# RWKV heads of a hybrid trunk: one standing PSUM tile for two banks, and output products in one queue behind the state update

## The chip, the cores and the metric

The kernel runs on one core of one Trainium2 chip. The metric is the device time of one execution in microseconds. The program uses TensorE (PE in the profile, its weight loads PEld), VectorE (DVE), ScalarE (ACT), GpSimd (POOL) and the DMA queues issued by SyncE (SP).

## The reference

One layer of a hybrid trunk over 4096 tokens of width 1024: h = RMSNorm(x), one projection of h whose columns feed three head groups, the group outputs concatenated, one output projection, RMSNorm, residual add.

- Mamba-2 group: 8 heads of 64, causal convolution, chunked scan, gated norm.
- RWKV-7 group: 4 heads of 64. Per head and token `S = S * w + (S a) b^T + v k^T` and `y = S r`, then a GroupNorm over the 64 channels of a head, a bonus and a SiLU gate.
- Memory attention group: 4 heads of 64 over 256 memory tokens.

```python
def step(S, inp):
    r_t, w_t, k_t, v_t, a_t, b_t = inp
    sa = jnp.einsum('bhij,bhj->bhi', S, a_t)
    S = S * w_t[:, :, None, :] + sa[..., None] * b_t[:, :, None, :] + v_t[..., None] * k_t[:, :, None, :]
    return S, jnp.einsum('bhij,bhj->bhi', S, r_t)
```

The change touches the RWKV group and the PSUM banks that the other two groups share with it.

## The kernel before

The tokens go in 16 stages of 256 (`NS = 16`, `NT = 256`). Three phases follow one another and overlap a little at their borders: phase A does the norm, the Mamba projections and the Mamba scan, phase B the RWKV projections and recurrence, phase C the attention, the output projection and the residual. Projections are split into a high and a low part in a reduced-precision fp32 format (three products for one, in `proj_cm`, L137, and `proj_tm`, L147); all else is plain fp32, and each plain fp32 product leaves two MATMUL records in the trace.

The RWKV recurrence is computed in chunks of 64 tokens, four per stage (`NC_`). Four heads lie as two pairs `p_`; the two heads `h` of a pair are the two halves of the 128 partitions. Per stage:

- `gram2` (L722) multiplies the stacked vectors of each chunk with each other, per head over that head's 64 rows (L730), into two PSUM banks, one for each head of the pair, and VectorE masks each bank into `AT` (L733). This is done for one pair, then for the other.
- `solve2` (L741) inverts small triangular blocks with many 32x32 products (L785, L793, L805, L815) into `TT`.
- `tokmaj` (L825) copies v, r and the scaled vectors into token-major tiles: `UV`, `rr` (L840) and `BKt` (L848).
- `stage3` (L861) is the recurrence: per chunk three groups of four products one after the other, L878, L885 and L895, with copies on ScalarE and VectorE in between (L871, L881, L890), and the state update `ST` on VectorE (L898). After every second chunk (a half stage) it emits 16 output products: step 0 multiplies the state with `rr` per head over 64 rows (L912), step 1 adds the product inside the chunk (L915).
- `stage4` (L922) is the GroupNorm: per head bank a mean (L927) and a subtraction (L931) out of PSUM.

There are eight PSUM banks: two for transposes (`tr`), two for projections (`pj`), one each for `g`, `yo`, `yd` and `st`. `yd` and `st` are the two head banks of `gram2` and of the output products. Phase A uses the same two for its scan (L425 and L417), phase C for the output projection (L1165).

`weave` (L95) runs generators in turns, by the numbers given with them, and so sets the order in which instructions are traced. A list scheduler of the language then sets the order on each engine from that order, the dependencies and its own timing model. An instruction without a dependency on its neighbour can therefore land anywhere between others. PE, DVE and ACT then run their own lists in that order. A PE product is described below by its shape, rows*columns of the array that it uses, as the profile prints it: 128*128 for projections, 128*64 for L878, L895 and L915, 64*64 for L885 and L912, 64*128 for L730 and 32*32 for the solve.

Of the kernel before, what the change touches and what calls it, by code (L numbers as in the profile page):

```python
# [7 lines left out]
F32 = mybir.dt.float32  # L8
# [6 lines left out]
P = 128  # L15
# [12 lines left out]
def tile_hymba_trunk(  # L28
# [17 lines left out]

    def psum(tag, bufs):
        return ps.tile([P, 512], F32, name="ps_" + tag, tag=tag, bufs=bufs)
# [444 lines left out]
    def phase_b(a_tail, a_l):  # L493
# [216 lines left out]
        nct = bi.tile([P, 16, 2 * NPC], F32, name="nct")  # L710
# [8 lines left out]
        rr = bw.tile([P, 2, NC_, C], F32, name="rr")  # L719
        el = bw.tile([P, 2, NC_], F32, name="el")  # L720

        def gram2(i, r):  # L722
            AR, BK, ec = r["AR"], r["BK"], r["ec"]
            AT = bi.tile([P, NPC, 2, P], F32, name="AT", tag="AT", bufs=2)
            for p_ in range(2):
                pas = (psum("g", 1), ps_tr()) if i == NS - 1 else (psum("yd", 1), psum("st", 1))
                for c_ in range(NC_):
                    for h, pa in enumerate(pas):
                        hs = slice(h * 64, h * 64 + 64)
                        te.matmul(pa[:, c_ * P:(c_ + 1) * P], lhsT=BK[hs, p_, c_].rearrange("p a t -> p (a t)"),  # L730
                                  rhs=AR[hs, p_, c_].rearrange("p a t -> p (a t)"), start=True, stop=True)
                for h, pa in enumerate(pas):
                    v.tensor_tensor(out=AT[:, p_ * NC_:(p_ + 1) * NC_, h, :], in0=pa.rearrange("p (x t) -> p x t", t=P),  # L733
                                    in1=amask.unsqueeze(1).broadcast_to([P, NC_, P]), op=ALU.mult)
                    yield

                g.tensor_tensor(out=BK[:, p_].rearrange("p c a t -> p c (a t)"), in0=BK[:, p_].rearrange("p c a t -> p c (a t)"),
                                in1=ec[:, p_].unsqueeze(2).broadcast_to([P, NC_, 2 * C]), op=ALU.mult)
            r.update(scaled=True, AT=AT)

        def solve2(i, r):  # L741
            AT = r["AT"]
            for q in range(4):
# [33 lines left out]
            Dt = bi.tile([P, NPC, 32], F32, name="Dt", tag="Dt")  # L777
# [47 lines left out]
        def tokmaj(r, c2):  # L825
# [14 lines left out]
            s.copy(out=rr[:, :, cs, :], in_=AR[:, :, cs, 1, :])  # L840
# [20 lines left out]
        def stage3(i, r, nxt=None):  # L861
# [3 lines left out]
            for c_ in range(NC_):  # L865
# [26 lines left out]
                for p_, pc in enumerate(pcs):  # L892
                    for h in range(2):
                        hs = slice(h * 64, h * 64 + 64)
                        te.matmul(pch[hs, 256 + p_ * C:256 + p_ * C + C], lhsT=BKt[:, pc, hs], rhs=UV[:, pc, h, :],  # L895
# [5 lines left out]
                if c_ % 2 == 1:  # L901
                    for step in range(2):
                        for p_ in range(2):
                            for h in range(2):
                                hs = slice(h * 64, h * 64 + 64)
                                for par in range(2):
# [4 lines left out]
                                    if step == 0:  # L911
                                        te.matmul(yo, lhsT=rr[hs, p_, cq, :], rhs=sts[cq][hs, p_, :], start=(p_ == 0), stop=False,  # L912
                                                  skip_group_check=True)
                                    else:
                                        te.matmul(yo, lhsT=AT[:, pc, h, C:2 * C], rhs=UV[:, pc, h, :], start=False, stop=True,  # L915
                                                  skip_group_check=True)
# [5 lines left out]
        def stage4(i, r):  # L922

            pys = r["py"]
            mean = bw.tile([P, 2, 4], F32, name="mean", tag="mean")
            for h in range(2):
                v.tensor_reduce(out=mean[:, h, :], in_=pys[h][:, 0:256].rearrange("p (c t) -> p c t", t=C), axis=AX.X, op=ALU.add)  # L927
            g.tensor_scalar(out=mean, in0=mean, scalar1=1.0 / C, scalar2=None, op0=ALU.mult)
            yc = bw.tile([P, NPC, C], F32, name="yc", tag="yc")
            for h in range(2):  # L930
                v.tensor_tensor(out=yc[:, h::2, :], in0=pys[h][:, 0:256].rearrange("p (c t) -> p c t", t=C),  # L931
                                in1=mean[:, h, :].unsqueeze(2).broadcast_to([P, 4, C]), op=ALU.subtract)
# [354 lines left out]
```

## Time and profile before

| what | us |
|---|---|
| median of 3 runs | 2287.77 (2286.9 to 2288.61) |
| the profiled execution | 2286.42 |
| its span | 2284.7 |
| PE busy | 2211.9 (97%) |
| DVE busy | 1444.0 (63%) |
| ACT busy | 1153.6 (50%) |
| first gram product (L730) | at 821.7 |
| last transposition of the RWKV output (L946) | at 1620.2 |

Busy shares come from the records of each engine. Records of PE overlap: a product is recorded until its results are out, while the next one has started. So the time that a product takes from the others is read from start to start and not from its duration. Idle time of an engine stands with what released it.

### The profile page before, as it was taken

The numbers are of one execution on the slowest core, as the hardware profiler recorded it, in microseconds if no ns is written. First come the engines' busy times: TensorE is split into PE (matmuls) and PEld (weight loads), VectorE is DVE, ScalarE is ACT, GpSimd is POOL, SyncE is SP. The second block draws the span as 40 slices with busy tenths as digits, with TensorE's granted clock in tenths as the row PEclk, the third lists the DMA queues.
The fourth block names the chain that finished last, engine by engine and source line by source line (L and its number), as shares of the span: only waits on it lengthen the run. The fifth ranks groups of instructions, "written<-read, shape, count | busy, mean of one in ns | idle before, by whom it ended". The sixth has DMA issues, their size and how long they took to land.

```text
span 2284.7 us, 54434 instructions
## 1 busy us (share of the span) xinstructions
PE 2211.9 (97%) x22497; PEld 2091.5 (92%) x22497; DVE 1444.0 (63%) x3298; ACT 1153.6 (50%) x2803; POOL 721.0 (32%) x1047
## 2 busy tenths in 40 slices
PE   4999999999999889999999999999999999999997
PEld 4999999999999889899898899988899999999997
DVE  5788888888888986677677777776533333323322
ACT  6555555545554655666666666676423323323322
POOL 1343444343433342333433343333121212211212
PEclk8999999999999999999999999999999999999999
DMA  6232223222332422111111111234524324324311
GB/s 199 84 137 96 93 94 136 97 93 94 128 105 103 128 69 75 48 43 43 43 67 56 48 43 43 73 110 144 185 94 147 116 89 148 116 89 147 117 47 56
DMA packets 83766, 219.60 MB, mean 96 GB/s; under 512 B 9207, under 2 KB 45502, under 8 KB 71230
## 3 DMA queue, kind: packets, MB, share of 16 engines
q1 hardware_dynamic: 82334, 215.59, 27.4%
q8 instruction: 177, 2.90, 0.5%
q10 hardware_dynamic: 1184, 0.53, 0.1%
q14 instruction: 71, 0.58, 0.1%
HBM read 152.52 MB, written 63.57 MB: 95 GB/s over the span
## 4 chain that ended last, share of the span: by engine, by line
PE 85%; DVE 5%; DMA 4%; ACT 2%; issue 1%; POOL 1%; SPq 0%; POOLq 0%; DVEq 0%; ACTq 0%
PE ps_pj L137 39%; PE ps_pj L147 8%; PE ps_st L147 8%; PE ps_yd L147 8%; PE ps_pj L1140 3%; DMA w_st<-in_w_in_dram 1%; PE ps_yd L425 1%; DVE cc L296 1%; PE ps_yo L878 1%; PE ps_tr L1128 1%; PE ps_yd L730 1%; PE ps_tr L126 1%; PE ps_st L417 1%; PE ps_yo L404 1%; PE ps_st L730 1%
## 5 line engine op out<-in xcount | busy, mean ns | idle before, releaser
L137 PE MATMUL ps_pj<-hh,w_hi 128*128 128x256 f32 x2704 | 789.2, 292 | 5.7 <-ACT w_hi L78 4.0
L137 PE MATMUL ps_pj<-hh,w_lo 128*128 128x256 f32 x2704 | 778.7, 288 | 2.0 <-DVE w_lo L79 1.9
L137 PE MATMUL ps_pj<-hl,w_hi 128*128 128x256 f32 x2704 | 778.0, 288 | 0.0
L137 PEld LDWEIGHTS ps_pj<-hh,w_hi 128*128 128x128 f32 x2704 | 519.4, 192 | 15.1 <-ACT w_hi L78 4.8
L137 PEld LDWEIGHTS ps_pj<-hh,w_lo 128*128 128x128 f32 x2704 | 519.1, 192 | 8.6 <-DVE w_lo L79 3.3
L137 PEld LDWEIGHTS ps_pj<-hl,w_hi 128*128 128x128 f32 x2704 | 519.4, 192 | 7.9 <-issue 2.2
L296 DVE SCALAR_TENSOR_TENSOR cc<-ux,cwh,cc 128x256 f32<-128x256 f32 x384 | 220.1, 616 | 15.2 <-ACT cc L293 11.3
L147 PE MATMUL ps_pj<-w_hi,hh 128*128 128x260 f32 (+1 forms) x528 | 155.4, 295 | 21.5 <-DVE dtr L270 17.2
L1174 POOL TENSOR_TENSOR sq<-sq 128x1 f32<-128x1 f32 x32 | 6.2, 194 | 496.5 <-ACT ot L1172 496.5
L147 PE MATMUL ps_pj<-w_hi,hl 128*128 128x260 f32 (+1 forms) x528 | 152.3, 289 | 0.0
L147 PE MATMUL ps_pj<-w_lo,hh 128*128 128x260 f32 (+1 forms) x528 | 151.3, 287 | 0.0
L147 PEld LDWEIGHTS ps_pj<-w_hi,hh 128*128 128x128 f32 x528 | 101.7, 193 | 24.0 <-issue 17.3
L147 PEld LDWEIGHTS ps_pj<-w_lo,hh 128*128 128x128 f32 x528 | 101.5, 192 | 0.2
L147 PEld LDWEIGHTS ps_pj<-w_hi,hl 128*128 128x128 f32 x528 | 101.4, 192 | 0.0
L1180 POOL TENSOR_TENSOR xr<-ot,xr 128x512 f32<-128x512 f32 x64 | 88.0, 1398 | 26.3 <-DVE ot L1179 26.3
L299 ACT ACTIVATE th<-cc 128x512 f32<-128x512 f32 x64 | 40.4, 632 | 104.1 <-DVE cc L296 101.9
L1179 DVE SCALAR_TENSOR_TENSOR ot<-ps_yd,sq,pnw 128x512 f32<-128x512 f32 x32 | 24.0, 751 | 104.9 <-POOL sq L1176 104.9
L1093 DVE TENSOR_TENSOR ylo<-yl,yh 128x512 fp32r<-128x512 f32 x48 | 35.5, 741 | 84.4 <-ACT yh L1092 84.1
L567 ACT ACTIVATE tt<-ps_pj,omu 128x256 f32<-128x256 f32 x144 | 68.1, 473 | 38.0 <-PE ps_pj L137 25.3
L385 POOL TENSOR_TENSOR xde<-xdt,de 128x512 f32<-128x512 f32 x32 | 46.7, 1459 | 123.3 <-DVE xdt L383 119.1
L147 PE MATMUL ps_yd<-wo0h,yh 128*128 128x256 f32 x256 | 75.8, 296 | 4.2 <-DVE ot L1179 2.8
L1144 DVE TENSOR_TENSOR sg<-ps_pj,sg 128x256 f32<-128x256 f32 x32 | 13.6, 424 | 104.0 <-PE ps_pj L1140 104.0
(453 smaller groups left out, 5891.4 us busy)
## 6 DMA issues: line engine op xcount, KB each, us to landing
hl<-hTd SPq DMA_DIRECT2D x32, 1024.0 KB
hh<-hTd SPq DMA_DIRECT2D x32, 1024.0 KB
xt<-in_x_dram SPq DMA_DIRECT2D x32, 512.0 KB
hTd<-hh SPq DMA_DIRECT2D x16, 1024.0 KB
hTd<-hl SPq DMA_DIRECT2D x16, 1024.0 KB
R<-rowd SPq DMA_DIRECT2D x32, 512.0 KB
xr<-in_x_dram SPq DMA_DIRECT2D x32, 512.0 KB
out_dram<-xr SPq DMA_DIRECT2D x32, 512.0 KB
```

Source lines behind the costliest of these rows:

```text
L126: te.transpose(pt[:, q * P:(q + 1) * P], src[:, k * P:(k + 1) * P], ident)
L137: te.matmul(outp, lhsT=a[:, k, :], rhs=b[:, k, :], start=(n == 0), stop=(n == 3 * KB - 1))
L147: te.matmul(outp, lhsT=a[:, k, tsl], rhs=b[:, k, 0:ncol], start=(n == 0), stop=(n == 3 * KB - 1))
L296: v.scalar_tensor_tensor(out=cc[:, b_, :], in0=ux[:, b_, j:j + NT], scalar=wj(j), in1=cc[:, b_, :], op0=ALU.mult, op1=ALU.add)
L299: s.activation(out=th, in_=cc, func=AF.Tanh)
L385: g.tensor_tensor(out=h3(xde), in0=h3(xdt), in1=b3(q[c]["de"]), op=ALU.mult)
L567: s.activation(out=tt[:, b_, :], in_=pv[:, b_, :], func=AF.Copy, scale=omu[:, m0 + b_:m0 + b_ + 1])
L730: te.matmul(pa[:, c_ * P:(c_ + 1) * P], lhsT=BK[hs, p_, c_].rearrange("p a t -> p (a t)"), rhs=AR[hs, p_, c_].rearrange("p a t -> p (a t)" ...
L1093: v.tensor_tensor(out=YL[:, bs, :], in0=yl, in1=YH[:, bs, :].bitcast(F32), op=ALU.subtract)
L1140: te.matmul(po[g_ * 64:g_ * 64 + 64, p_ * P:(p_ + 1) * P], lhsT=vm[:, m_, n_ * 64:n_ * 64 + 64], rhs=pT[:, p_, m_, :], start=(m_ == 0), st ...
L1179: v.scalar_tensor_tensor(out=ots[n_], in0=pos[n_], scalar=sq[:, 0:1], in1=pnw[:, cs], op0=ALU.mult, op1=ALU.mult)
L1180: g.tensor_tensor(out=xr[:, cs], in0=ots[n_], in1=xr[:, cs], op=ALU.add)
```

## The change

The two tags `yd` and `st` no longer come from the rotating pool. One tile `big` of two banks is allocated once, and `psum("yd", ...)` and `psum("st", ...)` return its two halves, in all three phases. With it:

- `gram2` masks both banks with one VectorE instruction over 1024 elements per partition, except in the last stage, which uses other banks.
- `stage4` takes the means with one reduction and subtracts with one instruction.
- `rr` is twice as large and cleared once; each head's r is copied into its own half of the partitions and its own slot, so that the other half of the rows is zero. The state product then contracts over all 128 rows.
- State product and output product of one destination follow each other, and all 16 of a half stage are traced inside `tc.issue_after(upd.ins)`: they stand behind the last product of the state update (L895 before, L908 now) on PE's list.
- `nct` and `Dt` take the buffers of `N` and `T`, which makes room.

```diff
+    big = ps.tile([P, 2, 512], F32, name="ps_big")
     def psum(tag, bufs):
+        if tag in ("yd", "st"):
+            return big[:, ("yd", "st").index(tag), :]
         return ps.tile([P, 512], F32, name="ps_" + tag, tag=tag, bufs=bufs)
...
-        nct = bi.tile([P, 16, 2 * NPC], F32, name="nct")
...
-        rr = bw.tile([P, 2, NC_, C], F32, name="rr")
+        rr = bw.tile([P, 2, 2, NC_, C], F32, name="rr")
+        v.memset(rr, 0.0)
...
-                for h, pa in enumerate(pas):
-                    v.tensor_tensor(out=AT[:, p_ * NC_:(p_ + 1) * NC_, h, :], in0=pa.rearrange("p (x t) -> p x t", t=P),
-                                    in1=amask.unsqueeze(1).broadcast_to([P, NC_, P]), op=ALU.mult)
-                    yield
+                if i == NS - 1:
...
+                else:
+                    v.tensor_tensor(out=AT[:, p_ * NC_:(p_ + 1) * NC_].rearrange("p x h t -> p h x t"),
+                                    in0=big.rearrange("p h (x t) -> p h x t", t=P),
+                                    in1=amask.unsqueeze(1).unsqueeze(1).broadcast_to([P, 2, NC_, P]), op=ALU.mult)
+                yield
+                yield
...
+            nct = bi.tile([P, 16, 2 * NPC], F32, name="nct", tag="N")
...
-            Dt = bi.tile([P, NPC, 32], F32, name="Dt", tag="Dt")
+            Dt = bi.tile([P, NPC, 32], F32, name="Dt", tag="T")
...
-            s.copy(out=rr[:, :, cs, :], in_=AR[:, :, cs, 1, :])
+            for h in range(2):
+                hs = slice(h * 64, h * 64 + 64)
+                s.copy(out=rr[hs, h, :, cs, :], in_=AR[hs, :, cs, 1, :])
...
-                        te.matmul(pch[hs, 256 + p_ * C:256 + p_ * C + C], lhsT=BKt[:, pc, hs], rhs=UV[:, pc, h, :],
+                        upd = te.matmul(pch[hs, 256 + p_ * C:256 + p_ * C + C], lhsT=BKt[:, pc, hs], rhs=UV[:, pc, h, :],
                                   start=True, stop=True)
...
-                    for step in range(2):
+                    with tc.issue_after(upd.ins):
                         for p_ in range(2):
                             for h in range(2):
-                                hs = slice(h * 64, h * 64 + 64)
                                 for par in range(2):
...
-                                    if step == 0:
-                                        te.matmul(yo, lhsT=rr[hs, p_, cq, :], rhs=sts[cq][hs, p_, :], start=(p_ == 0), stop=False,
-                                                  skip_group_check=True)
-                                    else:
-                                        te.matmul(yo, lhsT=AT[:, pc, h, C:2 * C], rhs=UV[:, pc, h, :], start=False, stop=True,
-                                                  skip_group_check=True)
+                                    te.matmul(yo, lhsT=rr[:, h, p_, cq, :], rhs=sts[cq][:, p_, :], start=True, stop=False)
+                                    te.matmul(yo, lhsT=AT[:, pc, h, C:2 * C], rhs=UV[:, pc, h, :], start=False, stop=True)
...
-            for h in range(2):
-                v.tensor_reduce(out=mean[:, h, :], in_=pys[h][:, 0:256].rearrange("p (c t) -> p c t", t=C), axis=AX.X, op=ALU.add)
+            pyv = big[:, :, 0:256].rearrange("p h (c t) -> p h c t", t=C)
+            v.tensor_reduce(out=mean, in_=pyv, axis=AX.X, op=ALU.add)
...
-            for h in range(2):
-                v.tensor_tensor(out=yc[:, h::2, :], in0=pys[h][:, 0:256].rearrange("p (c t) -> p c t", t=C),
-                                in1=mean[:, h, :].unsqueeze(2).broadcast_to([P, 4, C]), op=ALU.subtract)
+            v.tensor_tensor(out=yc.rearrange("p (c h) t -> p h c t", h=2), in0=pyv,
+                            in1=mean.unsqueeze(3).broadcast_to([P, 2, 4, C]), op=ALU.subtract)
```

How the order on PE moves: this is PE's list before at the end of the second chunk pair of a stage in the middle of phase B (`ps_yd` and `ps_st` are the two head banks, `ps_yo` the chunk's bank, `ps_pj` a projection's; the last numbers are partitions x elements of the result).

```order
L137 MATMUL ps_pj<-hl,w_hi 128x256
L912 MATMUL ps_yd<-ST,rr 64x64
L137 MATMUL ps_pj<-hh,w_lo 128x256
L912 MATMUL ps_st<-ST,rr 64x64
L912 MATMUL ps_yd<-ST,rr 64x64
L912 MATMUL ps_st<-ST,rr 64x64
L912 MATMUL ps_yd<-ST,rr 64x64 x2
L912 MATMUL ps_st<-ST,rr 64x64
L878 MATMUL ps_yo<-UV,AT 64x64 x4
L912 MATMUL ps_st<-ST,rr 64x64
L915 MATMUL ps_yd<-UV,AT 64x64
L915 MATMUL ps_st<-UV,AT 64x64
```

The eight state products stand in three pieces with a projection product and a chunk group in between, and two of the eight output products behind them; the other six follow in two pieces further on. Now the list of the change at the same place of a stage (its lines are 4 higher in the projections, 13 higher at the state update, and L923 and L924 stand for L912 and L915):

```order
L141 MATMUL ps_pj<-hl,w_hi 128x256
L141 MATMUL ps_pj<-hh,w_lo 128x256
L908 MATMUL ps_yo<-UV,BKt 64x64 x4
L923 MATMUL ps_big<-ST,rr 64x64
L924 MATMUL ps_big<-UV,AT 64x64
```

The last two rows repeat until each stands eight times, and then projection products follow. No other product stands between the state update and the last of the sixteen.

On DVE, before, around the masking of the gram products of a stage:

```order
L733 TENSOR_TENSOR AT<-ps_yd,amask 128x4x128
L733 TENSOR_TENSOR AT<-ps_st,amask 128x4x128
L939 TENSOR_TENSOR yc<-yc,var 128x512
L890 COPY UV<-ps_yo 64x2x64
L733 TENSOR_TENSOR AT<-ps_yd,amask 128x4x128
L733 TENSOR_TENSOR AT<-ps_st,amask 128x4x128
L898 TENSOR_TENSOR ST<-S_13639,ps_yo 128x128
```

and now:

```order
L741 TENSOR_TENSOR AT<-ps_big,amask 128x2x4x128
L945 TENSOR_TENSOR yc<-yc,var 128x512
L572 SCALAR_TENSOR_TENSOR tt<-ps_pj,pcol,tt 128x255
L575 TENSOR_TENSOR cm<-ps_pj,pcol 128x1
L903 COPY UV<-ps_yo 64x2x64
L588 TENSOR_TENSOR lt<-tt,lt 64x256 x2
L741 TENSOR_TENSOR AT<-ps_big,amask 128x2x4x128
L959 TENSOR_TENSOR t_13466<-t_13466,ug 128x512
L911 TENSOR_TENSOR ST<-S_13548,ps_yo 128x128
```

The four maskings of a stage are two, of twice the size. Counted over PE's whole list, the shape changes from one product to the next 980 times before and 772 times now: 84 and 85 up to the first gram product, 776 and 589 from there to the last transposition of the RWKV output, 120 and 98 behind it.

More of the change, by code (lines that the diff above doesn't have):

```diff
@@ L731, in gram2 @@
                                   rhs=AR[hs, p_, c_].rearrange("p a t -> p (a t)"), start=True, stop=True)
-                for h, pa in enumerate(pas):
-                    v.tensor_tensor(out=AT[:, p_ * NC_:(p_ + 1) * NC_, h, :], in0=pa.rearrange("p (x t) -> p x t", t=P),
-                                    in1=amask.unsqueeze(1).broadcast_to([P, NC_, P]), op=ALU.mult)
-                    yield
+                if i == NS - 1:
+                    for h, pa in enumerate(pas):
+                        v.tensor_tensor(out=AT[:, p_ * NC_:(p_ + 1) * NC_, h, :], in0=pa.rearrange("p (x t) -> p x t", t=P),
+                                        in1=amask.unsqueeze(1).broadcast_to([P, NC_, P]), op=ALU.mult)
+                else:
[4 more added lines that the diff above has]
+                yield
                 g.tensor_tensor(out=BK[:, p_].rearrange("p c a t -> p c (a t)"), in0=BK[:, p_].rearrange("p c a t -> p c (a t)"),
@@ L922, in stage4 @@
         def stage4(i, r):
-            pys = r["py"]
             mean = bw.tile([P, 2, 4], F32, name="mean", tag="mean")
-            for h in range(2):
-                v.tensor_reduce(out=mean[:, h, :], in_=pys[h][:, 0:256].rearrange("p (c t) -> p c t", t=C), axis=AX.X, op=ALU.add)
+            pyv = big[:, :, 0:256].rearrange("p h (c t) -> p h c t", t=C)
+            v.tensor_reduce(out=mean, in_=pyv, axis=AX.X, op=ALU.add)
             g.tensor_scalar(out=mean, in0=mean, scalar1=1.0 / C, scalar2=None, op0=ALU.mult)
             yc = bw.tile([P, NPC, C], F32, name="yc", tag="yc")
-            for h in range(2):
-                v.tensor_tensor(out=yc[:, h::2, :], in0=pys[h][:, 0:256].rearrange("p (c t) -> p c t", t=C),
-                                in1=mean[:, h, :].unsqueeze(2).broadcast_to([P, 4, C]), op=ALU.subtract)
+            v.tensor_tensor(out=yc.rearrange("p (c h) t -> p h c t", h=2), in0=pyv,
+                            in1=mean.unsqueeze(3).broadcast_to([P, 2, 4, C]), op=ALU.subtract)
             yq = bw.tile([P, NPC, C], F32, name="yq", tag="t512", bufs=2)
```

## The prediction

> **What bounds the kernel now.** I read the page's first part, then the busy time by stretches, then PE's waits, and last the instructions of PE in order of time.
>
> ```profile
> span 2284.7 us, 54434 instructions
> PE 2211.9 (97%) x22497; PEld 2091.5 (92%) x22497; DVE 1444.0 (63%) x3298; ACT 1153.6 (50%) x2803; POOL 721.0 (32%) x1047
> PE 85%; DVE 5%; DMA 4%; ACT 2%; issue 1%; POOL 1%; SPq 0%; POOLq 0%; DVEq 0%; ACTq 0%
> ```
>
> PE carries 85% of the chain that ended last, and no other engine is above 63% busy. Now by stretches (PE, PEld, DVE, ACT, POOL busy, clock, DMA):
>
> ```profile
> 300.00:400.00 100.00, 99.93 (x920) 97.02 (x919) 82.30 (x169) 53.41 (x120) 40.91 (x60) 1.00 0.35 123
> 1100.00:1200.00 100.00, 100.00 (x1371) 90.10 (x1371) 70.75 (x186) 66.51 (x163) 36.99 (x52) 1.00 0.18 65
> 1200.00:1300.00 100.00, 100.00 (x1315) 89.93 (x1316) 70.99 (x184) 64.72 (x160) 35.51 (x50) 1.00 0.14 54
> 1500.00:1600.00 100.00, 93.61 (x1233) 83.17 (x1232) 67.53 (x167) 67.87 (x169) 35.41 (x46) 0.98 0.39 133
> 821.70:1620.30 798.60, 784.29 (x10294) 708.03 (x10293) 558.39 (x1451) 515.71 (x1269) 282.37 (x388) 0.99 0.19 67
> ```
>
> The RWKV phase runs from the first gram product at 821.7 to the last transposition of its output at 1620.3. In its middle PE is 100% busy at full clock, yet its weight loads fall from 97 to 90%: a busy PE is doing something that is not streaming. It does not wait for other engines there; in the whole span PE's waits on the work that the change touches are these:
>
> ```profile
> PE ps_yd L147 <- DVE ot L1179: 2.8, 1, 2.8
> PE ps_yd L915 <- DVE UV L890: 1.8, 3, 0.7
> PE ps_yd L912 <- DVE ST L898: 0.9, 2, 0.5
> PE ps_st L912 <- DVE AT L733: 0.5, 1, 0.5
> ```
>
> So time in this phase is what PE's own sequence takes, and that has to be read from start to start. This is one half stage (start, duration, line; an fp32 product leaves two records, so x2 is one product and x8 four):
>
> ```profile
> 1208.83 0.28 PE L137 MATMUL ps_pj<-hh,w_hi 128*128 128x256 f32 x1
> 1208.95 0.28 PE L137 MATMUL ps_pj<-hl,w_hi 128*128 128x256 f32 x1
> 1209.16 0.32 PE L912 MATMUL ps_yd<-ST,rr 64*64 64x64 f32 x2
> 1209.42 0.38 PE L137 MATMUL ps_pj<-hh,w_lo 128*128 128x256 f32 x1
> 1209.73 0.27 PE L912 MATMUL ps_st<-ST,rr 64*64 64x64 f32 x1
> ...
> 1210.11 0.45 PE L878 MATMUL ps_yo<-UV,AT 128*64 128x64 f32 x8
> 1210.49 0.33 PE L912 MATMUL ps_st<-ST,rr 64*64 64x64 f32 x2
> 1210.74 0.33 PE L915 MATMUL ps_yd<-UV,AT 128*64 128x64 f32 x2
> 1210.91 0.28 PE L915 MATMUL ps_st<-UV,AT 128*64 128x64 f32 x2
> 1211.12 0.39 PE L137 MATMUL ps_pj<-hh,w_hi 128*128 128x256 f32 x1
> 1211.34 0.28 PE L137 MATMUL ps_pj<-hl,w_hi 128*128 128x256 f32 x1
> ...
> 1216.75 0.28 PE L137 MATMUL ps_pj<-hh,w_hi 128*128 128x256 f32 x1
> 1216.96 0.45 PE L915 MATMUL ps_yd<-UV,AT 128*64 128x64 f32 x6
> 1217.33 0.38 PE L137 MATMUL ps_pj<-hl,w_hi 128*128 128x256 f32 x1
> 1217.56 0.27 PE L137 MATMUL ps_pj<-hh,w_lo 128*128 128x256 f32 x1
> ...
> 1217.99 0.45 PE L895 MATMUL ps_yo<-UV,BKt 128*64 128x64 f32 x8
> 1218.28 0.40 PE L915 MATMUL ps_st<-UV,AT 128*64 128x64 f32 x6
> 1218.61 0.39 PE L137 MATMUL ps_pj<-hh,w_lo 128*128 128x256 f32 x1
> ```
>
> Two projection products of L137 start 0.12 us apart (1208.83, 1208.95). Before a product whose rows*columns differ the step is 0.21 (1208.95 to 1209.16): +0.09. Behind the first product after a return it is 0.22 (1211.12 to 1211.34): +0.10. The piece in between pays as well: four products with another shape behind them take 0.38 (L878, 1210.11), four with the same shape behind them 0.29 (L895, 1217.99), so leaving costs 0.09; three products take 0.37 as a piece of their own (1216.96) and 0.33 appended to L895 (1218.28), so entering costs 0.04. One excursion from L137 into another shape and back thus costs 0.09+0.10+0.04+0.09, about 0.33 us beyond its work, or 0.165 for each change of shape. PE's order has 980 such changes, 776 of them in the RWKV phase.
>
> **The change part by part.**
>
> *Output products, the main term.* A half stage has 8 state products (L912) and 8 output products (L915). Above they stand in six pieces; over the 32 half stages the order has 195 pieces (98 of L912, 97 of L915), 6.1 each, so this is a typical one. Their own time is 0.26 (1209.16) + 0.38 (1209.73) + 0.25 (1210.49) + 0.38 (1210.74) + 0.37 (1216.96) + 0.33 (1218.28) = 1.97. L137 pays around the two excursions that exist for them alone: 0.19 at 1209.16, and 0.09 + 0.11 at 1216.96 (leaving 0.21, the return 1217.33 to 1217.56 0.23). The others share theirs with L878 and L895, which remain. Before: 2.36 us.
>
> Now all sixteen have one shape, 128*64, the shape of L895, and stand right behind it: no entering, one leaving of 0.09. Four products whose column halves alternate take 0.29 with entering, so a pair in different halves costs 0.12; a product that cannot pair costs 0.12 alone (1210.91 to 1211.12 is 0.21 with a leaving of 0.09). In the new order the half changes at 7 of 15 steps: 7 pairs and 2 single ones, 9 x 0.12 = 1.08, with leaving 1.17. If no pair overlapped, 16 x 0.12 + 0.09 = 2.01. The gain per half stage is 1.19, at worst 0.35; times 32, 38 us, at worst 11. I take the overlap, since L878 and L895 show it in the same shape.
>
> Contracting over 128 rows gives up the four-way packing of L912: six of its products took 0.38 at 1209.73, as long as four of L878, so without the 0.13 for entering and leaving 0.04 each against 0.06; 256 of them, 5 us, are in the 1.08 already. On the Trainium skill's page "TensorEngine Tiling (Array Packing)", section "Theoretical Speedup", a small dimension of at most 64 promises up to twofold speed from tiling, which speaks against this edit; by that alone the state products would lose, and the sum would be 5 us over the time before instead of below it. The same page's "Key Properties" let a change of mode drain the engine, and the 0.21 against 0.12 above agrees.
>
> *The whole phase, counted.* The merged gram eviction lets the eight gram products stand closer (47 pieces, 61 before), and the rest shifts both ways. Changes of shape in the phase go from 776 to 589. 187 x 0.165 = 31 us. The tally gives 38, the count 31; I take **35**. Outside, the attention and output phase goes from 120 to 98 changes: 22 x 0.165, **4 us**, at worst nothing, since only the order moved there. The Mamba phase has 84 and 85: nothing.
>
> *Evictions.* Four rows price them, with the two copies of `rr`:
>
> ```profile
> L733 DVE TENSOR_TENSOR AT<-ps_yd,amask 128x512 f32<-128x512 f32 x30 | 20.6, 688 | 13.8 <-PE ps_yd L730 12.5 <-PE ps_st L730 1.2
> L363 DVE TENSOR_TENSOR R<-R,acs 128x1024 f32<-128x1024 f32 x32 | 38.9, 1217 | 0.1
> L931 DVE TENSOR_TENSOR yc<-ps_yd,mean x16: 409/425/427, 903.9 to 1613.1; 128x256 f32<-128x256 f32 x16
> L840 ACT COPY rr<-AR 128x256 f32<-128x256 f32 x32 | 13.4, 421 | 0.3
> L818 ACT COPY TT<-Dt 32x256 f32<-32x256 f32 x32 | 12.9, 404 | 5.0 <-DVE Dt L795 4.4
> ```
>
> Two of 0.69 become one of about 1.22 (an estimate from L363): DVE saves 0.15 x 30, about 5 us. The two reductions and the two subtractions of some 0.42 become two of about 0.69: 0.3 x 16, another 5. ACT's copy of `rr`, 0.42, becomes two of about 0.41 (L818 has as many elements per partition on a quarter of the rows): +13 us. All lies under PE, with DVE near 71% and ACT near 66% busy; uncovered it would be -10 and +13 us. Clearing the doubled `rr` once is at most 1.2 us (L363), in the ramp where PE is not full: **+1**. `nct` in N's buffer and `Dt` in T's reuse tiles whose last reader stands earlier in the same solve: nothing.
>
> *What is queued behind the block.* The next chunk's L878 needs the state sum on DVE and two copies on ACT after L895:
>
> ```profile
> L898 DVE TENSOR_TENSOR ST<-S,ps_yo 128x128 f32<-128x128 f32 x64 | 18.3, 286 | 32.3 <-PE ps_yo L895 24.6 <-ACT UV L837 5.1 <-PE ps_st L915 1.8
> L871 ACT COPY UV<-ST 64x128 f32<-64x128 f32 x128 | 37.9, 296 | 21.9 <-DVE ST L898 20.1
> ```
>
> 0.29 + 2 x 0.30 = 0.88 us, so a block of 1.08 to 1.92 delays it by at most 1 us, and L137 stands between them anyway.
>
> *Sum.* The profiled execution took 2286.42, its span 2284.7 and 1.7 around it. 2286.4 - 35 - 4 + 1 = 2248.4; it lies 1.35 below the median of 2287.77, so **2250 us**.
>
> **The rivals.**
>
> *No overlap in the block.* Two products into one column half follow each other, and the pairing across them may fail. For: L915 at 1210.74 and 1210.91 ran one after the other in one half. Against: L895's four in 0.29. Then 11 + 4 us remain: 2273.
>
> *The standing tile stalls PE (slower).* Both halves are now released together. Gram products wait for the one subtraction of stage 4, or for the one 1.22 us eviction of the gram half before, and everything on PE queues behind them. In the new order mostly 30 to 44 PE products lie between the two gram halves of a stage, about 28 of them L137's, so 28 x 0.12 = 3.4 us of cover. DVE must be more than 3.4 - 1.2 = 2.2 us behind for any loss; at 3.7 us behind, the 30 halves lose 1.5 us each, 45 us, and 2250 becomes 2295. For: DVE is in order and 71% busy. Against: the waits quoted above name DVE's AT once, with 0.5 us.
>
> *PE is not the bound.* If its busy record hides idle time, the changes of shape saved are waited away again: 2288. For: ends of products are modelled. Against: the steps of 0.12 are as regular as rows get.
>
> *The page's rule alone.* If changes of shape were free and only packing counted: 2287.8 + 5 = 2293. Against: the 0.33 us per excursion, read directly.
>
> **How the numbers follow.** Forecast 0.78, no overlap 0.09, stalls 0.06, not the bound 0.05, the rule alone 0.02. The forecast's own range is 2238 to 2262: 38 + 4 and shorter ramps below, 31 with nothing in the last phase and a few us of new waits above. Up to 2276 it takes in the block without overlap and leaves out 0.13. Under 0.2%, 4.6 us, a measurement cannot tell a change from none. Faster is 0.78 + 0.09 = 0.87, same 0.05, slower 0.06 + 0.02 = 0.08.
>
> **What would show it.** In the stretches 1100 to 1300 the projection products per 100 us rise and PEld's busy share rises from 90% to some 92%. In PE's order of time each L895 of an odd chunk is followed at once by 32 records of the two product lines, from start to start about 1.1 us, then L137. The gram row of 1024 elements is near 1.2 us. PE's waits on DVE's AT and yc stay under some 3 us. I would be wrong if the block takes 1.9 us, if PE gains waits of ten us or more on `big`, or if the phase from first gram to last transposition does not shrink by some 35 us from 798.6.

## The result, and the profile after

The changed kernel is slower: 2348.45 us median (2343.65 to 2352.96) against 2288.19 beside it, a ratio of 1.026 (1.024 to 1.029). The forecast was 2250, with 2276 as its upper end. The profiled execution is the shortest of the four, 2343.65. Its page, first part and chain:

```profile
PE 2205.3 (94%) x22497; PEld 2099.0 (90%) x22497; DVE 1455.0 (62%) x3237; ACT 1158.9 (49%) x2835; POOL 715.6 (31%) x1047
PE 67%; DVE 13%; ACT 9%; DMA 6%; issue 3%; POOL 2%; POOLq 0%; ACTq 0%; SPq 0%; DVEq 0%
```

PE's busy time fell by 6.6 us, but the span grew by 57.2, from 2284.7 to 2341.9, and PE's share of the chain fell from 85 to 67%, with ACT and DVE in its place. The busy time by stretches (length, PE, PEld, DVE, ACT, POOL busy, clock, DMA) puts it into two phases. First the last phase before, then the RWKV phase, the last phase and the middle of the RWKV phase after:

```profile
1620.30:2284.70 664.40, 651.14 (x5327) 631.10 (x5325) 224.85 (x448) 200.26 (x544) 131.15 (x218) 0.99 0.33 111
```

```profile
823.40:1634.60 811.20, 767.23 (x10282) 704.03 (x10282) 570.13 (x1399) 530.30 (x1303) 291.29 (x394) 0.95 0.18 65
1634.60:2341.90 707.30, 660.92 (x5321) 637.66 (x5319) 225.18 (x447) 196.55 (x543) 128.00 (x218) 0.98 0.31 105
1200.00:1300.00 100.00, 96.62 (x1359) 88.58 (x1357) 70.54 (x173) 66.95 (x165) 36.89 (x50) 0.95 0.15 52
```

- Up to the first gram product: 821.7 before, 823.4 after, +1.7.
- RWKV phase: 798.6 to 811.2, **+12.6** where -35 was forecast. PE's busy time there fell by 17.1 (784.29 to 767.23), and its idle time rose by 29.7 (14.3 to 44.0). The granted clock went from 0.99 to 0.95.
- Attention and output phase: 664.4 to 707.3, **+42.9** where -4 was forecast. PE's idle time rose by 33.1 (13.3 to 46.4), its busy time by 9.8.

So three quarters of the loss lie in a phase whose code the change hardly touches. PE's waits there, after (total, times, longest):

```profile
PE ps_pj L1146 <- ACT pT L1135: 23.5, 15, 2.2
PE ps_big L151 <- DVE ot L1185: 10.0, 16, 4.0
```

The second row before was 2.8 us, once (L147 on L1179, quoted in the prediction). The place in order of time, on PE and DVE (start, duration, line; the bracket is idle time and what ended it):

```profile
1778.34 1.41 DVE L1185 SCALAR_TENSOR_TENSOR ot<-ps_big,sq,pnw 128x512 f32<-128x512 f32 x2 [8.55 <-POOL sq L1182]
...
1779.31 0.28 PE L1116 MATMUL ps_yo<-kl,qs 128*128 128x256 f32 x1
1779.81 0.39 PE L151 MATMUL ps_big<-wo0h,yh 128*128 128x256 f32 x1 [0.22 <-DVE ot L1185]
```

The DVE row is two readings, one of each half of `big` (0.7 us each, in turn), and ends at 1779.75. The first product of the next tile, `wo0h`, writes the first half, which the first reading had left about 0.7 us earlier. It starts 0.06 us after the *second* reading has ended. When `yd` was a tile of its own, its one reader released it. The Mamba phase shows the same across the halves. There `yd`'s product L429 waits for VectorE's `prev`, which reads the other half, `st`; the kernel before has no such wait:

```profile
PE ps_big L429 <- DVE prev L423: 6.3, 8, 2.0
```

That phase grew by 1.7 us in all.

The larger row, L1146, is not on `big` at all. In order of time:

```profile
1931.82 0.47 ACT L1120 ACTIVATE pr<-ps_yo,mx 128x256 f32<-128x256 f32 x1
1932.27 0.59 ACT L1135 COPY pT<-ps_tr 128x512 f32<-128x512 f32 x1
1932.91 1.09 PE L1146 MATMUL ps_pj<-pT,vm 128*64 128x128 f32 x8 [1.94 <-ACT pT L1135]
1933.93 0.38 PE L151 MATMUL ps_big<-wo0h,yh 128*128 128x256 f32 x1
```

The attention's value products L1146 now stand on PE's list ahead of the tile's first output product, and wait 1.94 us for a copy that stands on ACT behind other work. Before, the output products stood there, right behind the score products (L147 at 1928.04, with no wait); now they come behind L1146. That the list scheduler arranges PE around the later release of `big` is a reading which the first experiment tests.

The larger waits of the RWKV phase after, and the two that a rival had named:

```profile
PE ps_pj L141 <- DVE cm L575: 9.1, 5, 5.8
PE ps_yo L898 <- ACT X L894: 7.7, 9, 1.6
PE ps_tr L844 <- ACT UV L848: 6.7, 5, 1.7
PE ps_yo L908 <- ACT UV L903: 6.0, 7, 1.1
PE ps_yo L891 <- ACT UV L884: 5.7, 6, 3.8
PE ps_big L151 <- DVE yc L937: 1.4, 1, 1.4
PE ps_big L734 <- DVE AT L741: 0.9, 1, 0.9
```

The first row is a projection that waits for its bank; 5.8 of its 9.1 us are one wait that ends 30 us after the first gram product, and the kernel before has no such row. The next four rows, on ACT's copies of the recurrence, make 26.1 us. Before, the copies X (L881) and UV (L871) made PE wait 1.0 and 0.2 us, and the row on the copy L890 was this:

```profile
PE ps_yo L895 <- ACT UV L890: 1.9, 3, 1.1
```

The waits that the rival of the standing tile had named, on AT (gram) and yc (stage 4), are 0.9 and 1.4. One of the places, in order of time:

```profile
1279.48 0.25 ACT L848 COPY UV<-ps_tr 64x128 f32<-64x128 f32 x1
1279.76 0.41 ACT L853 COPY rr<-AR 64x256 f32<-64x256 f32 x1
1280.19 0.54 ACT L848 COPY UV<-ps_tr 64x128 f32<-64x128 f32 x2
1280.76 0.40 ACT L853 COPY rr<-AR 64x256 f32<-64x256 f32 x1
1281.18 0.26 ACT L848 COPY UV<-ps_tr 64x128 f32<-64x128 f32 x1
1281.50 0.44 PE L844 MATMUL ps_tr<-ident,uv 128*128 128x128 f32 x2 [1.43 <-ACT UV L848]
```

The two `rr` copies (0.41 and 0.40) stand *between* the UV copies that PE's next transposition waits for. ACT runs the five rows without a pause, so the last UV copy ends 0.8 us later than it would without them, and PE waits 1.43 us. The same stretch in slices, with the clock in the third column from the right:

```profile
1279.30:1282.70 3.40, 1.65 (x16) 1.13 (x14) 1.49 (x3) 3.25 (x10) 1.73 (x2) 0.99 0.00 0
1282.70:1292.90 10.20, 8.57 (x176) 7.85 (x178) 8.31 (x17) 4.60 (x13) 6.78 (x8) 0.50 0.01 2
```

PE is busy 1.65 of 3.40 us, and then its clock is halved for 10.2 us: a wait of 1.4 us is followed by up to 5.1 us of lost work. Over the span the mean granted clock went from 0.986 to 0.971. Lost clock time, (1 - clock) x span, went from 32 to 68 us. What of these 36 us is loss of time and what falls into idle time anyway, the rows don't say.

### The profile page after: what moved, and what is told of

The parts are those of the page before. It is cut to its first block, busy times and chain, and to the rows that moved or that the text cites. A ratio compares the mean times of both kernels' runs of the same rounds, so it can differ in the third digit from the quotient of the medians.

```text
span 2341.9 us, 54384 instructions
## 1 busy us (share of the span) xinstructions
PE 2205.3 (94%) x22497; PEld 2099.0 (90%) x22497; DVE 1455.0 (62%) x3237; ACT 1158.9 (49%) x2835; POOL 715.6 (31%) x1047
## 4 chain that ended last, share of the span: by engine, by line
PE 67%; DVE 13%; ACT 9%; DMA 6%; issue 3%; POOL 2%; POOLq 0%; ACTq 0%; SPq 0%; DVEq 0%
PE ps_pj L141 27%; PE ps_big L151 16%; PE ps_pj L151 8%; DVE cc L300 4%; DMA R<-rowd 2%; PE ps_pj L1146 2%; DMA xt<-in_x_dram 2%; PE ps_big L734 1%; PE ps_big L429 1%; ACT ot L1178 1%; DVE ot L1185 1%; DVE t L775 1%; PE ps_yo L891 1%; ACT nct L757 1%; ACT w_hi L82 1%
## 5 line engine op out<-in xcount | busy, mean ns | idle before, releaser
L151 PE MATMUL ps_pj<-w_hi,hh 128*128 128x260 f32 (+1 forms) x528 | 157.1, 298 | 20.3 <-DVE dtr L274 16.3
L151 PE MATMUL ps_pj<-w_lo,hh 128*128 128x260 f32 (+1 forms) x528 | 151.6, 287 | 0.8 <-POOL w_lo L88 0.7
L151 PE MATMUL ps_pj<-w_hi,hl 128*128 128x260 f32 (+1 forms) x528 | 152.2, 288 | 0.0
L1185 DVE SCALAR_TENSOR_TENSOR ot<-ps_big,sq,pnw 128x512 f32<-128x512 f32 x64 | 45.0, 744 | 141.9 <-POOL sq L1182 135.8
L151 PEld LDWEIGHTS ps_pj<-w_hi,hh 128*128 128x128 f32 x528 | 102.0, 193 | 22.3 <-issue 16.5
L1178 ACT ACTIVATE ot<-ps_big 128x512 f32<-128x512 f32 x64 | 37.6, 594 | 158.1 <-PE ps_big L151 158.1
L151 PEld LDWEIGHTS ps_pj<-w_lo,hh 128*128 128x128 f32 x528 | 101.7, 193 | 1.2 <-POOL w_lo L88 1.1
L151 PEld LDWEIGHTS ps_pj<-w_hi,hl 128*128 128x128 f32 x528 | 101.5, 192 | 0.0
L1146 PE MATMUL ps_pj<-pT,vm 128*64 128x128 f32 x512 | 70.1, 280 | 24.1 <-ACT pT L1135 23.9
L1186 POOL TENSOR_TENSOR xr<-ot,xr 128x512 f32<-128x512 f32 x64 | 82.7, 1317 | 31.3 <-DVE ot L1185 31.3
L151 PE MATMUL ps_big<-wo0h,yh 128*128 128x256 f32 x256 | 81.1, 317 | 11.4 <-DVE ot L1185 10.0
```

What stands on the lines that cost most here:

```text
L151: te.matmul(outp, lhsT=a[:, k, tsl], rhs=b[:, k, 0:ncol], start=(n == 0), stop=(n == 3 * KB - 1))
L1146: te.matmul(po[g_ * 64:g_ * 64 + 64, p_ * P:(p_ + 1) * P], lhsT=vm[:, m_, n_ * 64:n_ * 64 + 64], rhs=pT[:, p_, m_, :], start=(m_ == 0), st ...
L1178: s.activation(out=ot, in_=pos[n_], func=AF.Square, accum_out=sq[:, n_:n_ + 1])
L1185: v.scalar_tensor_tensor(out=ots[n_], in0=pos[n_], scalar=sq[:, 0:1], in1=pnw[:, cs], op0=ALU.mult, op1=ALU.mult)
L1186: g.tensor_tensor(out=xr[:, cs], in0=ots[n_], in1=xr[:, cs], op=ALU.add)
```

## The experiments

Theories at the start. **W**: the dependence goes by the whole two-bank tile, so a half waits for the other half's reader, most of all in the output phase. **G**: the queue itself lengthens the recurrence, since the output products no longer fill PE's waits. **A**: ACT's extra copies sit in the recurrence. The expectations, written as the runs went along, call A also L, and Q is G and A together. Every run made from the changed kernel keeps the shared buffers of `nct` and `Dt`.

### Which part of the change costs

**Tile only in the RWKV phase.** The change, with the two-bank tile there alone; phases A and C take two one-bank tiles from a pool.

```diff
-    big = ps.tile([P, 2, 512], F32, name="ps_big")
+    def own_banks(name):
...
+        own["big"] = own["pool"].tile([P, 2, 512], F32, name="ps_big") if name == "psB" else None
...
         if tag in ("yd", "st"):
-            return big[:, ("yd", "st").index(tag), :]
+            if own["big"] is not None:
+                return own["big"][:, ("yd", "st").index(tag), :]
+            return own["pool"].tile([P, 512], F32, name="ps_" + tag, tag=tag, bufs=bufs)
...
```

> The change, but the two-bank tile lives only in the RWKV phase; the Mamba and the output phase take their two banks from the pool as before. Theory W (whole tile: a product into one half of the standing tile waits for readers of the other half, so the output phase lost its 43 us, 664.4 to 707.3, to waits and to the clock that falls in them): the output phase returns to about 664 us, PE's waits on DVE ot and ACT pT there fall from 34 us to some 3, and the time comes to about 2348 - 43 - 2 = 2303. Rival S (the standing tile is harmless, the output phase slows because of what the RWKV phase leaves behind, its new order and the lower clock): the output phase stays near 707 us, the time near 2348.

Measured: 2293.78 us, ratio 1.0027 (1.0017 to 1.0037). The stretch of the last phase, three of PE's waits in the RWKV phase, and the value products' wait in the last phase (L1157 and L1146 stand for L1146 and L1135):

```profile
1627.00:2292.60 665.60, 651.67 (x5327) 631.47 (x5325) 223.49 (x447) 199.62 (x543) 131.19 (x218) 0.99 0.33 111
```

```profile
PE ps_yo L919 <- ACT UV L914: 12.5, 11, 4.0
PE ps_yo L909 <- ACT X L905: 8.0, 10, 1.3
PE ps_yo L902 <- ACT UV L895: 4.7, 4, 1.7
```

```profile
PE ps_pj L1157 <- ACT pT L1146: 0.7, 2, 0.4
```

The last phase is back at 665.6, its value products wait 0.7 us instead of 23.5, and its output products wait for `ot` 2.8 us, once, as before. That is W, with the secondary effect on the order included: 41.7 of the 42.9 us go with the shared tile. The RWKV phase takes 803.9 us, against 811.2 and 798.6. So 7.3 us of its loss go with the tile in the phases around it; PE's wait on `cm` falls there from 9.1 to 2.2 us.

**Queue only.** The change with pool banks and separate evictions: 128-row state products, paired and queued, and two `rr` copies. The edit is shown against the kernel before.

```diff
-        rr = bw.tile([P, 2, NC_, C], F32, name="rr")
+        rr = bw.tile([P, 2, 2, NC_, C], F32, name="rr")
...
-                    for step in range(2):
+                    with tc.issue_after(upd.ins):
...
+                                    te.matmul(yo, lhsT=rr[:, h, p_, cq, :], rhs=sts[cq][:, p_, :], start=True, stop=False)
+                                    te.matmul(yo, lhsT=AT[:, pc, h, C:2 * C], rhs=UV[:, pc, h, :], start=False, stop=True)
```

> The kernel before with one part of the change alone: the state products contract over 128 rows, paired with the output products in one queue behind the state update; the two banks come from the pool and keep their separate evictions. If the saved changes of shape are a gain and the waits in the RWKV phase come from the tile and its merged evictions: the RWKV phase falls from 798.6 by some 30 us and the time to about 2258. Rival Q (the waits of the RWKV phase, 40 us and more, come from the queue itself: a block of 1.1 us ahead of the next chunk and 13 us more of copies on ACT in the recurrence): the RWKV phase stays at 805 to 815 us and the time at 2290 to 2300.

Measured: 2290.76, ratio 1.0013 (0.9994 to 1.0032): no change. Its RWKV phase, two of PE's waits, and one place (ACT and PE, in order of time):

```profile
822.90:1622.30 799.40, 770.68 (x10298) 706.05 (x10298) 570.43 (x1452) 530.45 (x1302) 288.43 (x388) 0.96 0.19 66
```

```profile
PE ps_yo L898 <- ACT UV L893: 9.7, 10, 1.3
PE ps_yo L888 <- ACT X L884: 5.3, 13, 0.7
```

```profile
1275.58 0.47 ACT L567 ACTIVATE tt<-ps_pj,omu 128x256 f32<-128x256 f32 x1 [0.55 <-DVE uv L568]
1276.07 0.26 ACT L893 COPY UV<-ps_yo 64x128 f32<-64x128 f32 x1
1276.39 0.45 PE L898 MATMUL ps_yo<-UV,BKt 128*64 128x64 f32 x8 [1.29 <-ACT UV L893]
```

```profile
1273.80:1277.20 3.40, 2.11 (x132) 1.78 (x134) 1.69 (x5) 1.47 (x4) 3.40 (x2) 1.00 0.00 0
1277.20:1284.00 6.80, 6.75 (x72) 6.27 (x60) 6.64 (x14) 2.28 (x6) 4.15 (x7) 0.50 0.01 2
```

PE's busy time fell by 13.6 us (784.29 to 770.68) although its clock was lower; the length stayed the same. A 0.47 us projection eviction of ACT, itself held up 0.55 us by DVE, stands ahead of the UV copy that the state update waits for, PE idles 1.29 us, and the clock halves for 6.8 us. The gain was made and waited away again: W has no part in this kernel.

**Tile only.** The change without the queue, in the old shapes and with the old `rr`.

```diff
-                    with tc.issue_after(upd.ins):
+                    for step in range(2):
...
-                                    te.matmul(yo, lhsT=rr[:, h, p_, cq, :], rhs=sts[cq][:, p_, :], start=True, stop=False)
+                                    if step == 0:
+                                        te.matmul(yo, lhsT=rr[hs, p_, cq, :], rhs=sts[cq][hs, p_, :], start=(p_ == 0), stop=False,
...
```

> The change without the queue: the standing tile with its merged evictions, but state and output products in the old shapes and order. Theory W: the output phase shows the full loss, about 705 us. In the RWKV phase, if the queue makes the waits (Q), it is below 798.6, near 785, and the time about 2318; if the tile makes them, it is 820 or more and the time 2350 or more.

Measured: 2350.82, ratio 1.0275 (1.0256 to 1.0294), as long as the change itself. Its last phase:

```profile
1637.70:2351.90 714.20, 665.51 (x5327) 642.19 (x5325) 225.44 (x447) 196.36 (x543) 126.82 (x218) 0.98 0.31 104
```

Against the kernel before, the tile costs 49.8 us here, and 16.6 in the RWKV phase too (815.2 us, between the two values expected). 6.7 us of PE's waits there are on `cm`, as in the change.

**Two standing tiles.** The kernel before, with two one-bank tiles allocated once.

```diff
+    alone = {tag: ps.tile([P, 512], F32, name="ps_" + tag) for tag in ("yd", "st")}
+
     def psum(tag, bufs):
+        if tag in alone:
+            return alone[tag]
```

> The kernel before with two standing one-bank tiles in place of the pool's two banks, all evictions and products as before. Theory W (it is the common tile, not that it stands): nothing changes, 2288 within 5 us, the output phase near 664. Rival P (a standing tile loses something that the pool's rotation gives): the output phase slows as in the change, 2325 to 2335.

Measured: 2286.4, ratio 0.9999 (0.9989 to 1.0009). The last phase took 666.1 us. Standing does no harm; being *one* tile does.

### What ate the gain of the queue

**The `rr` copies on GpSimd**, in the queue-only kernel:

```diff
-                s.copy(out=rr[hs, h, :, cs, :], in_=AR[hs, :, cs, 1, :])
+                g.tensor_copy(out=rr[hs, h, :, cs, :], in_=AR[hs, :, cs, 1, :])
```

> The queue-only kernel of 2290.8 us (RWKV phase 799.4 us, of which about 31 us are lost to a halved clock), with the two copies of rr per half stage on GpSimd instead of ScalarE. Theory L (ACT's load: 13 us more of copies push back the copies of the recurrence): PE's waits on ACT UV and ACT X in the phase, 18 us, fall to a few, the clock stays up, and the phase comes to some 775 us, the time to 2266. Theory G (one gap per two stages: in each 95 us PE stands some 1.5 us before a state update product, behind a projection's eviction that stands ahead of the UV copy on ACT, and the clock then halves for 3 to 10 us; the rr copies are elsewhere): the gaps stay, 2286 to 2294.

Measured: 2278.94, ratio 0.9966 (0.9953 to 0.9979). The RWKV phase went from 799.4 to 789.4, the wait on the X copy from 5.3 to 1.6 us and that on the UV copy from 9.7 to 7.4. The gain is smaller than A had led me to expect (2266), so A holds in part.

**128-row pairs without the queue**, so that the scheduler may spread them:

```diff
-                    with tc.issue_after(upd.ins):
+                    if True:
```

> The queue-only kernel without its queue: state products over 128 rows, paired with the output products, but free to be placed anywhere. PE's order then has 754 changes of shape in the RWKV phase, 776 before and 601 with the queue. If the changes of shape set PE's own time and the queue makes the new waits: the phase near 795 us with the waits and the clock of the kernel before, 2284 within 5 us. If the contraction over 128 rows or the copies of rr make the waits: the waits on ACT UV and X are as long as with the queue, and the phase is above 810, the time above 2300.

Measured: 2289.0, ratio 1.0005 (0.9996 to 1.0015); I expected 2284. Its RWKV phase:

```profile
822.10:1622.00 799.90, 782.57 (x10296) 706.67 (x10295) 549.34 (x1452) 531.51 (x1303) 278.78 (x388) 0.99 0.19 67
```

```profile
PE ps_yo L898 <- ACT UV L893: 0.2, 1, 0.2
```

PE is busy nearly as before (782.57 us for 784.29), and the clock is 0.99 as it was. The wait on the UV copy is 0.2 us, where the same kernel with the queue has 9.7. So it is the queue that makes PE wait there, and two `rr` copies on ACT cost nothing that shows where the output products stay spread. With the queue and without it the phase has the same length: the queue trades PE's changes of shape for waits and clock.

**The queue alone, in the old shapes**, on the kernel before:

```diff
-                        te.matmul(pch[hs, 256 + p_ * C:256 + p_ * C + C], lhsT=BKt[:, pc, hs], rhs=UV[:, pc, h, :],
+                        upd = te.matmul(pch[hs, 256 + p_ * C:256 + p_ * C + C], lhsT=BKt[:, pc, hs], rhs=UV[:, pc, h, :],
...
+                    q_.enter_context(tc.issue_after(upd.ins))
                     for step in range(2):
...
```

> The kernel before with issue_after alone: state products over 64 rows first, then output products, all sixteen behind the state update; rr and its copy as before. PE's order has 682 changes of shape in the RWKV phase. Theory G: the gain of fewer changes, 94 x 0.165 = 15 us, is lost again where the queue leaves nothing to fill a wait, with gaps above 1 us and clock falls that the kernel before does not have: 2283 to 2292. If the queue does not make the waits but the new contraction does: no new gaps, the phase near 783, 2272.

Measured: 2279.85, ratio 0.9972 (0.9960 to 0.9984); RWKV phase 790.0. One `rr` copy on ACT instead of two, and the queue gains some 7 us without any 128-row product, half of the 15 expected from its fewer changes of shape. G in its strong form, that a queue must lose all that it saves, falls.

**Both UV copies on DVE**, in the queue-only kernel, so that no ACT eviction can stand ahead of one:

```diff
-                    (s.copy if h else v.tensor_copy)(out=UV[hs, c_::NC_, h, :],
+                    v.tensor_copy(out=UV[hs, c_::NC_, h, :],
```

> The queue-only kernel with both UV copies behind the solve product on VectorE (one was on ScalarE, where a projection's eviction stands ahead of it). Theory G: the gap of 1.5 us per two stages before the update product goes, the five clock falls between 1080 and 1470 us with it, and the phase comes to 770 to 780 us, the time to about 2265. If the gap is not what brings the clock down, the waits on ACT UV go and the halved clock stays: about 2283.

Measured: 2283.71, ratio 0.9983 (0.9974 to 0.9992); I expected 2265. PE's waits in its RWKV phase:

```profile
PE ps_yo L898 <- DVE UV L893: 7.2, 9, 1.1
PE ps_yo L881 <- ACT UV L874: 6.0, 5, 2.9
```

The wait moved with the copy, 9.7 us on ACT to 7.2 on DVE, and the copy L874 is waited for 6.0 us, where it was 2.7 without this edit. Any of the recurrence's copies can be late, not one engine's.

### Putting it together

**The change mended**: the tile only in the RWKV phase (as in the first run), and the `rr` copies on GpSimd.

```diff
-                s.copy(out=rr[hs, h, :, cs, :], in_=AR[hs, :, cs, 1, :])
+                g.tensor_copy(out=rr[hs, h, :, cs, :], in_=AR[hs, :, cs, 1, :])
```

> The whole change in the RWKV phase (queue, 128 rows, two-bank tile with merged evictions), its two banks in the other phases from the pool, and the rr copies on GpSimd: two repairs together. PE's order has 595 changes of shape in the phase. If the repairs add up (the pool alone brought 2349 to 2294, the copies on GpSimd 2291 to 2279 without the tile): 2282. If the merged evictions gain once ACT is relieved: 2272. If the longer eviction holds DVE up: 2288 or more.

Measured: **2263.69** (2262.18 to 2266.6), ratio 0.9896 (0.9882 to 0.9911), the fastest of all and below each of the three numbers expected for it. Its stretches and its waits:

```profile
822.00:1597.50 775.50, 750.20 (x10292) 688.59 (x10292) 558.21 (x1392) 505.75 (x1239) 311.05 (x453) 0.98 0.19 69
1200.00:1300.00 100.00, 99.72 (x1381) 91.41 (x1381) 75.83 (x198) 68.69 (x170) 41.86 (x63) 1.00 0.14 49
```

```profile
PE ps_yo L902 <- ACT UV L895: 4.2, 2, 3.4
PE ps_yo L919 <- ACT UV L914: 4.0, 8, 0.9
PE ps_yo L909 <- ACT X L905: 2.5, 4, 1.2
```

The middle is 99.72% busy at full clock again, with 1381 PE records in these 100 us where the kernel before had 1315 (1363 and 1371 in the 100 us ahead of them). The three waits fell from 25.2 to 10.7 us. The RWKV phase is 775.5, 23.1 below before: 34.1 us less of PE's work, 11.0 more idle.

**The old-shape queue with `rr` on GpSimd**, to see whether these 7 us and the 12 that the edit brought the queue-only kernel add up:

```diff
-            s.copy(out=rr[:, :, cs, :], in_=AR[:, :, cs, 1, :])
+            g.tensor_copy(out=rr[:, :, cs, :], in_=AR[:, :, cs, 1, :])
```

> The queue with the old shapes (2279.9 us) and the copy of rr on GpSimd. Theory G: PE's order is at 645 changes of shape against 682, 6 us less; waits on ACT somewhat shorter: 2270 to 2276. If the queue's own rigidity sets the loss: 2280.

Measured: 2284.97, ratio 0.999 (0.998 to 1.000). They do not: PE's wait on the UV copy grew from 6.5 us (8 times) without this edit to 10.1 (15 times) with it, although ACT has less to do. Every edit has the scheduler order all engines anew, and that shifts waits by several us either way. A gain of 7 us in one such kernel is no proof of a mechanism.

**`rr` on GpSimd alone**, on the kernel before, with the same edit:

```diff
-            s.copy(out=rr[:, :, cs, :], in_=AR[:, :, cs, 1, :])
+            g.tensor_copy(out=rr[:, :, cs, :], in_=AR[:, :, cs, 1, :])
```

> The kernel before with the copy of rr on GpSimd and nothing else. If the gain of rr on GpSimd is that it relieves the chain behind the queue: no change here, 2287 within 4 us, since PE hardly waits there. If it is a gain of its own: 2275 to 2280.

Measured: 2288.49, ratio 1.0003 (0.9993 to 1.0012). In this kernel PE hardly waits for ACT, and taking work off ACT is worth nothing.

**The change as it is, with `rr` on GpSimd**, the fourth corner of a square:

```diff
-                s.copy(out=rr[hs, h, :, cs, :], in_=AR[hs, :, cs, 1, :])
+                g.tensor_copy(out=rr[hs, h, :, cs, :], in_=AR[hs, :, cs, 1, :])
```

> The change with the rr copies on GpSimd alone; the standing tile serves all three phases. It completes a square with the change (2348), the tile in the RWKV phase only (2294) and both repairs (2264). If the two repairs act on different places, the whole-tile waits in the output phase and the waits on ACT in the RWKV phase: the output phase stays above 700 us, the RWKV phase comes to some 780, the time to 2316. If the rr copies repair the output phase too: below 2290. If they help only with the tile confined: above 2335.

Measured: 2315.5 (2312.36 to 2321.37), ratio 1.0137 (1.0112 to 1.0162). The last phase, untouched by this edit, stays long, and the RWKV phase falls from 811.2 to 784.1:

```profile
1609.50:2311.70 702.20, 657.18 (x5326) 634.34 (x5324) 225.07 (x447) 196.74 (x543) 128.70 (x218) 0.99 0.31 105
```

The square of medians, in us:

| | tile in all phases | tile in the RWKV phase | the tile elsewhere costs |
|---|---|---|---|
| two `rr` copies on ACT | 2348.45 | 2293.78 | 54.7 |
| two `rr` copies on GpSimd | 2315.5 | 2263.69 | 51.8 |
| the copies on ACT cost | 33.0 | 30.1 | |

The two losses add up within 3 us, so they are two causes and not one. The 30 to 33 us are what moving the copies is worth in these two kernels, the new order included, and not a price of the copies as such: the same edit brought 12 us in the queue-only kernel. The tile in the RWKV phase is what does not add. With the copies on ACT it costs 3 us against pool banks (2290.76 to 2293.78), with them on GpSimd it gains 15 (2278.94 to 2263.69).

## Why the prediction was wrong

Step by step, as it put them.

*PE's own time: right.* The block of sixteen products was put at 1.17 us with its leaving. After, in order of time:

```profile
1298.68 0.34 PE L923 MATMUL ps_big<-ST,rr 128*64 128x64 f32 x4
...
1299.76 0.38 PE L826 MATMUL ps_g<-Dt,p 32*32 32x32 f32 x12
```

From 1298.68 to 1299.76 it is 1.08, leaving included, so the rival without overlap (2.01) is out here. The term of 35 us is best read in the mended kernel, where little else disturbs it: PE's busy time in the phase fell by 34.1. With a clock lower by 0.01, some 8 us of lost work that the old clock would have saved, the fall lies between 34 and 42. The prediction's two ways of counting gave 31 and 38. The old-shape queue alone, with 94 fewer changes of shape, lowers PE's busy time there by 22.8. Both speak against the rival of the rule alone (2293), in which changes of shape are free.

*Evictions and copies: the sizes right, the cover wrong.* Groups of DVE and ACT in the RWKV phase after:

```profile
L741 DVE TENSOR_TENSOR AT<-ps_big,amask 128x1024 f32<-128x1024 f32 x30 | 36.4, 1214 | 3.1 <-PE ps_big L734 2.7
L853 ACT COPY rr<-AR 64x256 f32<-64x256 f32 x64 | 25.8, 404 | 1.3
```

1.22 and 0.41 had been forecast. But the sentence "All lies under PE, with DVE near 71% and ACT near 66% busy" holds **the first step that failed**. A busy share tells nothing of the place: the copies stand between those that PE's recurrence waits for, as the rows at 1279.76 and 1280.76 show. The prediction gave the price if uncovered as 13 us, the copies' own time. Taking both copies off ACT brought 30 to 33 in the square (25.8 us of work, of which ACT had 13.4 before as one copy) and 12 in the queue-only kernel; what the added half costs alone was not measured. At the place shown the copy is late, what stands behind it is late, and the halved clock follows. How much of the 30 is waiting and how much is clock was not separated by a run.

*The same cover, taken away from both sides.* The prediction noted that the next chunk's first group is delayed "by at most 1 us, and L137 stands between them anyway". In the old order the state and output products were also what PE did while ACT copied. Packing them into one place took that filling away, and PE reaches the next group of the recurrence sooner. The queue-only kernel shows it against its twin without the queue: 9.7 us on the UV copy against 0.2. Once PE is no longer the bound at such a place, a shorter PE piece gains nothing there. The rival "PE is not the bound" (2288) describes that kernel, at 2290.76, but for another reason than it gave: PE's record hid no idle time before; it gained it. That the number fits is luck.

*The output phase: the second step that failed, and the larger one.* "4 us, at worst nothing, since only the order moved there." It came to 42.9 us lost. Not only the order moved: the unit of release did. The change of the `psum` function applies to all phases, and the prediction priced the new wait only for the two merged evictions.

*The rival of the standing tile (2295, chance 0.06)* had the right sign and the wrong place; that its 45 us are near the 42.9 of the output phase is luck. It put the loss on gram products waiting for the one eviction and on stage 4; those waits are 0.9 and 1.4 us, below the 3 us that the forecast allowed. Its own sentence, "Both halves are now released together", holds with more force where nothing was merged: in the output phase each half has its own reader, and the first half is wanted while the second is still being read. Every PE product queued there waits, and the scheduler orders PE around it.

*The signs.* PEld's share in the middle was to rise from 90 to 92%; it fell to 88.58% in 1200 to 1300, and the mended kernel has 91.41. The projection products were to rise; from 1100 to 1300 they fell from 907 to 882. Of the three points named as refuting, two came: a wait of ten us on `big` (10.0, L151), and a phase that did not shrink. The block did not.

**What stays open.** Why the tile alone costs 16.6 us in the RWKV phase. The sharing with the other phases accounts for some 7 to 9 of them, if it costs there what it does in the square (811.2 to 803.9, 784.1 to 775.5); whether the shared buffers of `nct` and `Dt` have a part was not run. Why, on the other hand, with the queue and `rr` on GpSimd the tile goes with a phase 13.9 us *shorter* than the pool banks give (775.5 against 789.4). And why the old-shape queue gains 7 us and loses most of it with less work on ACT: the order is made anew each time, and no run held it fixed.

## What to carry to other kernels

Before two buffers become one, list for *every* phase that uses them who reads which half and who wants it next: the dependence goes by the tile, so a half now also waits for the other's reader, and a scheduler may move other work in front of that wait. Confine such a tile to the phase where both halves have one reader, and measure it there as well: here it gained or lost by what else stood in the phase. And before a helper engine's extra copy is costed at nothing because the engine is two thirds busy, look at what stands directly behind it on that engine and whether the bounding engine waits for it.

## What the runs showed of the hardware

The clock is more touchy than the shares suggest. A slice of 3.40 us with PE busy 1.65 (1279.3) or 2.11 us (1273.8, in the queue-only kernel) was followed by 10.2 and 6.8 us at 0.50, though PE was 96.62% busy in the 100 us from 1200 on, which hold the first of them. Between 1000 and 1500 us the changed kernel has four such falls and the queue-only kernel five, each behind 3.4 us in which PE was 39 to 67% busy; one slice of 65% in the changed kernel had no fall behind it. The Trainium skill's page "TensorE: Matmul & The Clock Gate", in "Part 1: The HAM clock gate", puts the fall behind at least one idle window of about 3.4 us. The halving and the lengths, two and three times 3.4, agree with it. That the window has to be idle does not: the longest waits in these two slices were 1.43 and 1.29 us.

One merged eviction saved what it should: 1.214 us for 0.688 and 0.681. DVE as a whole did not get lighter, though. Its busy time rose from 1444.0 to 1455.0 us. Two rows of the solve, the same number of instructions in the same shapes (L764 and L766 before, L775 and L777 after), rose from 102.8 to 114.5 us; why, stays open.
